# The expert passes' output stores are issued by GpSimd instead of the Activation engine

## The chip, the cores and the metric

The kernel runs on one core of one Trainium2 chip. The metric is device time in microseconds (us), the median of three runs. TensorE (PE) does the matmuls, VectorE (DVE) and the Activation engine (ACT) the elementwise work, GpSimd (POOL) some elementwise work and the indirect DMAs, and SyncE (SP) issues nearly all plain DMAs. All DMAs are carried by the same 16 DMA engines of the core; the profile counts them by queue: q1 holds what SP issues, q10 what ACT issues, q0 what GpSimd issues.

## What is computed

One decoder layer on 512 tokens of 1024 features: a mixer (mLSTM heads beside sliding-window attention heads), a layer norm, a hierarchical mixture of experts, a second layer norm. The part that the change touches is the mixture of experts, after the routing has picked two of 32 experts for each token:

```python
    for e in range(N_EXPERTS):
        h = jax.nn.silu(xt @ w_exp_gate[e]) * (xt @ w_exp_up[e])
        out = out + combine[:, e:e + 1] * (h @ w_exp_down[e])
    return out.reshape(B, S, Dm)
...
        x = layer_norm(ALPHA * x + y, ln2_w[l], ln2_b[l])
```

Everything is float32. The three weight tensors of the experts (1 MB each for one expert) are 101 MB together, and each is read once.

## The kernel before

The span has two stages. In the first, up to about 268 us, the mixer, the first norm and the routing run. In the second the experts run in 13 passes, numbered 0 to 12 (`ORDER = "BBBABABACBBCC"`). A pass gathers up to 128 token slots and serves two experts (kinds A and B) or four (kind C). For each pass TensorE forms the gate and up products of all its experts (`gu_part`, L1094), ACT and DVE make the hidden tile `hid` (`pair_h`, L1107 and L1108), TensorE transposes it (`dn_t`) and forms the down products `yo` (`dn_mm`, L1125). TensorE runs a pass's down products behind the next pass's gate and up products.

The results of passes 0 to 10 go to a DRAM buffer `yd`: `y_store` copies the two halves of `yo` to a tile `y` on ACT (L1142), scaled by the routing weight, and stores `y` (512 KB) by a DMA (L1143). Ahead of pass 11, `y_gather` fetches each token's two rows from `yd` with eight indirect DMAs of GpSimd (L1150), and DVE adds them to the residual `x1` (L1152). The results of passes 11 and 12 do not go through DRAM. Behind the eight adds in DVE's order stand the hidden tile of pass 11 and half of the copies that make the input `xs` of pass 12 (L1013).

The weights come in through a ring of 16 tiles of 1 MB, `we` (and two smaller buffers used once). `prefetch` (L624) takes free ring tiles in order and issues the loads of the next pass's weights from SP, two of 512 KB for gate and up (L597) or one of 1 MB for down (L601). A load waits until TensorE has read what its ring tile held before. `release` gives a pass's tiles back in a fixed order.

Which semaphore a DMA uses sets a second wait. The program has eight semaphores, DMAHW0 to DMAHW7, for the DMAs that SP and ACT issue, and eight, DMASW0 to DMASW7, for GpSimd's. They are dealt out in turn, in program order, and the next DMA on a semaphore waits at its issuing engine until the one before on that semaphore has landed. SP's queue is in order: what stands behind a waiting load waits too.

Of the kernel before, what the change touches and what calls it, by code (L numbers as in the profile page):

```python
# [24 lines left out]
P = 128  # L25
# [54 lines left out]
def layer_kernel(ctx, tc, x, w_in, conv_w, conv_b, gate_bias, norm_w, sinks, w_out, ln1_w, ln1_b,  # L80
# [3 lines left out]
    V, A, G, TE, SP = nc.vector, nc.scalar, nc.gpsimd, nc.tensor, nc.sync  # L84
# [16 lines left out]
    def slot(name, dt=F32, pool=None):  # L101
        _, p_, n = pools[pool or ("front" if name in FRONT else "mix")]
        return p_.tile([P, n], dt, tag="s", name=name)
# [29 lines left out]
    yd = DR.tile([KEPT * P + 1, DM], F32, name="yd")  # L133
# [998 lines left out]
    def y_split(py, cs, yh, yl):  # L1132
        for u in range(2):
            us = slice(512 * u, 512 * u + 512)
            A.activation(yh[:, us], py[u], AF.Copy, scale=cs)
            V.scalar_tensor_tensor(yl[:, us], py[u], cs, yh[:, us], op0=OP.mult, op1=OP.subtract)
        return yh, yl

    def y_store(py, p):
        y = slot("y")[:, :DM]  # L1140
        for u in range(2):
            A.activation(y[:, 512 * u:512 * u + 512], py[u], AF.Copy, scale=cws[:, p:p + 1])  # L1142
        A.dma_start(yd[p * P:(p + 1) * P], y)  # L1143


    def y_gather():
# [7 lines left out]
    def y_slots():  # L1154
        return [slot(n, F32R)[:, :DM] for n in ("yh", "yl")]
# [353 lines left out]
    for n, t in (("eid", eid), ("cwt", cwt), ("idf", idf), ("rank", rank)):  # L1509
        show(n, t)  # L1510

    y_store(pys[0], 0)
    xs = taken(2, hn)
    for d in range(2):
# [3 lines left out]
    hn = ready(4)  # L1518
    pg2 = pass_gu(xs, 0, 2)
    y_store(pys[1], 1)  # L1520
    prev = None
    l2 = []
# [28 lines left out]
    with tc.manual_schedule(engines={ENG.PE}):  # L1551
        for p in range(2, NP - 1):
            release(p, False)
            if p > 2:
                release(p - 1, True)
            prefetch(99)
            early = p in EARLY
            if early:
                y_store(pass_dn(dn_t(prev), p - 1), p - 1)
                y_gather()  # L1560
            hts = []
            pg = pg2 if p == 2 else pass_gu(xs, p % 2, p, (lambda: hts.append(dn_t(prev))) if prev and not early else None)
            if hts:
                ht = hts[0]
            h = pair_h(pg)
            if p % 2:
                xs = taken(p + 1, hn)
                if p + 3 < NP:
                    hn = ready(p + 3)
            if prev and not early:  # L1570
                y_store(pass_dn(ht, p - 1), p - 1)
            prev = h
# [45 lines left out]
    p = NP - 1  # L1618
# [4 lines left out]
    with tc.manual_schedule(engines=MAN):  # L1623
# [26 lines left out]
        y = y_split(py, cws[:, p - 1:p], *y_slots())  # L1650
# [133 lines left out]
```

## Time and profile before

| | |
|---|---|
| time, median of 3 runs (lowest, highest) | 553.78 us (550.93, 553.79) |
| time of the profiled execution | 549.58 us |
| its span from first to last instruction | 547.7 us |
| busy: PE, PEld, DVE, ACT, POOL | 478.3, 311.9, 257.3, 162.5, 146.5 us |
| DMA: read, written, mean rate | 128.68 MB, 10.49 MB, 254 GB/s |
| stores of `y` in q10 | 11 of 512 KB, 5.77 MB |

All times of events below are in us from the start of the span. The profiled execution lies 4.2 us under the median. Busy time alone does not show what a stage waits for: between 268 and 520 us the DMA engines move near their highest rate, and TensorE's busy share varies with what has been loaded. PEclk is the clock granted to TensorE, in tenths of its full 2.4 GHz.

### The profile page before, as it was taken

Reading aid. Unit: us, or ns where it says so; the run is one execution under the profiler, and the core shown is the slowest. Engines: PE = TensorE matmul, PEld = TensorE weight load, DVE = VectorE, ACT = ScalarE, POOL = GpSimd, SP = SyncE. Lnnn points to the kernel's source line nnn. Section 1 sums busy time; section 2 is a strip of 40 time slices with the busy share of each in tenths; the row PEclk is TensorE's granted clock in tenths of the full one; section 3 lists DMA queues with packets and bytes.
Section 4 is the critical chain, followed back from the end, with each engine's and each line's share of the span. In section 5 each row is a group of like instructions: output and inputs, shape, how many; then the busy total and the mean of one; then the engine's idle time right before and its main releaser. Section 6 shows DMA issues by size and latency. Waiting matters only on the chain. (4 is left out here: it accounts for less than half of the span.)

```text
span 547.7 us, 8113 instructions
## 1 busy us (share of the span) xinstructions
PE 478.3 (87%) x2904; PEld 311.9 (57%) x2904; DVE 257.3 (47%) x589; ACT 162.5 (30%) x352; POOL 146.5 (27%) x167
## 2 busy tenths in 40 slices
PE   6999899999999999797899999969478997287991
PEld 6998688798989878586447333216012631043330
DVE  3543898964487755978661103003000300324784
ACT  3552475874542512333202112202010211010520
POOL 4489724302311104646502000000000003201361
PEclk9999999999999999987999999989876997577996
DMA  8644213205936553759298998999799998999904
GB/s 229 198 117 116 78 34 94 77 30 158 414 89 185 193 149 133 276 193 376 80 394 323 405 425 335 394 390 373 245 418 333 404 347 307 411 421 413 424 29 172
DMA packets 44906, 139.42 MB, mean 255 GB/s; under 512 B 6386, under 2 KB 17674, under 8 KB 41024
## 3 DMA queue, kind: packets, MB, share of 16 engines
q1 hardware_dynamic: 40944, 126.05, 63.2%
q0 software_dynamic: 2336, 7.07, 3.5%
q10 hardware_dynamic: 1584, 5.77, 2.6%
q8 instruction: 24, 0.39, 0.3%
q14 instruction: 18, 0.15, 0.1%
HBM read 128.68 MB, written 10.49 MB: 254 GB/s over the span
## 5 line engine op out<-in xcount | busy, mean ns | idle before, releaser
L1094 PE MATMUL pg<-we,xs 128*32 128x512 f32 (+1 forms) x608 | 125.6, 674 | 33.7 <-DMA we<-in_w_exp_up 33.7
L1094 PEld LDWEIGHTS pg<-we,xs 128*32 128x32 f32 (+1 forms) x608 | 30.5, 129 | 114.2 <-issue 103.4
L245 PE MATMUL pj<-wh,xh 128*128 128x256 f32 (+1 forms) x224 | 63.2, 285 | 1.3 <-ACT wh L190 1.3
L246 PE MATMUL pj<-wh,xl 128*128 128x256 f32 (+1 forms) x224 | 62.4, 281 | 0.0
L1117 DVE COPY ht<-ph 128x256 f32<-128x256 f32 x13 | 5.5, 423 | 106.7 <-PE ph L1115 106.7
L250 PE MATMUL pj<-wl,xh 128*128 128x256 f32 x192 | 52.5, 280 | 0.0
L1150 POOL DMA_INDIRECT yg<-yd,yrow x8 | 7.5, 937 | 163.0 <-DMA yd<-y 153.5
L1125 PE MATMUL yo<-we,ht 128*32 128x512 f32 (+1 forms) x304 | 47.4, 595 | 2.1 <-DVE ht L1117 1.5
L1107 ACT ACTIVATE hid<-pg 128x256 f32<-128x256 f32 x13 | 5.0, 384 | 149.1 <-PE pg L1094 142.3
L1007 PE MATMUL xp<-ohr,x1h 128*128 128x256 f32 (+1 forms) x160 | 41.3, 297 | 5.9 <-DVE xs L1013 3.6
L245 PEld LDWEIGHTS pj<-wh,xh 128*128 128x128 f32 x224 | 42.1, 188 | 1.5 <-ACT wh L190 1.5
L246 PEld LDWEIGHTS pj<-wh,xl 128*128 128x128 f32 x224 | 42.1, 188 | 0.0
L1007 PE MATMUL xp<-ohr,x1l 128*128 128x256 f32 (+1 forms) x160 | 40.4, 292 | 0.0
L1007 PEld LDWEIGHTS xp<-ohr,x1h 128*128 128x128 f32 x160 | 32.2, 201 | 10.4 <-issue 5.2
L250 PEld LDWEIGHTS pj<-wl,xh 128*128 128x128 f32 x192 | 35.6, 188 | 0.0
L1007 PEld LDWEIGHTS xp<-ohr,x1l 128*128 128x128 f32 x160 | 32.3, 202 | 0.0
L191 DVE TENSOR_TENSOR wl<-wraw,wh 128x1024 fp32r<-128x1024 f32 x14 | 20.3, 1464 | 23.8 <-ACT wh L190 23.8
L1125 PEld LDWEIGHTS yo<-we,ht 128*32 128x32 f32 (+1 forms) x304 | 14.4, 119 | 29.0 <-issue 24.5
L190 ACT ACTIVATE wh<-wraw 128x1024 fp32r<-128x1024 f32 (+2 forms) x23 | 23.2, 1021 | 12.8 <-PE pj L246 4.2
L1152 DVE TENSOR_TENSOR x<-x,yg 128x1024 f32<-128x1024 f32 x8 | 9.9, 1239 | 35.1 <-DMA yg<-yd,yrow 35.1
L194 PE MATMUL pj<-xh,wh 128*128 128x512 f32 x64 | 25.7, 402 | 0.0
L196 PE MATMUL pj<-xl,wh 128*128 128x512 f32 x64 | 25.5, 399 | 0.0
(362 smaller groups left out, 913.5 us busy)
## 6 DMA issues: line engine op xcount, KB each, us to landing
we<-in_w_exp_gate SPq DMA_DIRECT2D x64, 512.0 KB
we<-in_w_exp_up SPq DMA_DIRECT2D x64, 512.0 KB
we<-in_w_exp_down SPq DMA_DIRECT2D x30, 1024.0 KB
wraw<-in_w_in SPq DMA_DIRECT2D x20, 512.0 KB
yd<-y ACTq DMA_DIRECT2D x11, 512.0 KB
xc<-in_x SPq DMA_DIRECT2D x4, 512.0 KB
wo<-in_w_out SPq DMA_DIRECT2D x8, 256.0 KB
wo<-in_w_out SPq DMA_DIRECT2D x4, 512.0 KB
```

Of the source, the lines that this page charges most:

```text
L190: A.activation(hi, src, AF.Copy)
L191: eng.tensor_tensor(lo, src, hi, op=OP.subtract)
L194: TE.matmul(o, lh, rh, start=start, stop=False)
L196: TE.matmul(o, lh, rl, start=False, stop=stop)
L245: TE.matmul(o, xh[j // 2][:, j % 2, cs], ws[i][j][0], start=j == 0, stop=False)
L246: TE.matmul(o, xl[j // 2][:, j % 2, cs], ws[i][j][0], start=False, stop=False)
L250: TE.matmul(o, xh[k // 2][:, k % 2, cs], ws[i][k][1], start=False, stop=k == 7)
L1007: TE.matmul(p_[:, j2, 0:P * n], w[c][:, 2 * g + j2], o[:, c, 0:P * n], start=c == 0 and s == 0 and j2 == 0, stop=c == NCH - 1 and s == 1 a ...
L1094: TE.matmul(pg[s:s + n], xs[k // 4][:, k % 4, P * b + s:P * b + s + n], ws[e][k // 4][:, :, k % 4], start=k == 0, stop=k == 7)
L1125: TE.matmul(py[u][s:s + n], ht[:, j, s:s + n], wt[e][2][j][:, 512 * u:512 * u + 512], start=j == 0, stop=j == 1)
L1150: G.indirect_dma_start(out=t, out_offset=None, in_=yd[:, :], in_offset=bass.IndirectOffsetOnAxis(ap=yrow[:, 2 * c + k:2 * c + k + 1], axis=0))
L1152: V.tensor_add(x1[c], x1[c], t)
```

## The change

One word: the DMA of L1143 is issued from GpSimd's queue (`G`) instead of ACT's (`A`).

```diff
@@ -1140,7 +1140,7 @@
         y = slot("y")[:, :DM]
         for u in range(2):
             A.activation(y[:, 512 * u:512 * u + 512], py[u], AF.Copy, scale=cws[:, p:p + 1])
-        A.dma_start(yd[p * P:(p + 1) * P], y)
+        G.dma_start(yd[p * P:(p + 1) * P], y)
```

On GpSimd, in the stretch from the last work of the first stage to the final norm, the eleven stores now stand between and behind the four gathers `xg<-xd` (the input rows of passes 4 to 7) and ahead of the eight gathers `yg<-yd`:

```order
 L1508 TENSOR_SCALAR x_2227<-x_2227 128x1024
-L1050 DMA xg<-xd,row 128x1024 x4
+L1143 DMA yd<-y 128x1024
+L1050 DMA xg<-xd,row 128x1024 x2
+L1143 DMA yd<-y 128x1024
+L1050 DMA xg<-xd,row 128x1024 x2
+L1143 DMA yd<-y 128x1024 x9
 L1150 DMA yg<-yd,yrow 128x1024 x8
 L1535 TENSOR_TENSOR l2d<-l2w,pcol 16x512 x2
```

The two gathers `xg` of passes 6 and 7 moved behind the second store, and the gathers `yg` stay behind all of them. Nothing else of GpSimd moved.

On SP no instruction moved, but the semaphores did. These are SP's loads of pass 3's down weights and of pass 4's gate and up weights, before; the wait named on a load is for the earlier DMA on its own semaphore and for TensorE's last read of the ring tile:

```order
L597 DMA we<-in_w_exp_up 128x1024 [waits DMAHW6_49]
L601 ISA
L601 DMA we<-in_w_exp_down 128x2048 [waits DMAHW0_49,PE_49]
...
L597 DMA we<-in_w_exp_gate 128x1024 [waits DMAHW5_49,PE_49]
L597 ISA
L597 DMA we<-in_w_exp_up 128x1024 [waits DMAHW6_49]
L597 ISA
L597 DMA we<-in_w_exp_gate 128x1024 [waits DMAHW7_49,PE_49]
```

The same loads in the changed kernel:

```order
L597 DMA we<-in_w_exp_up 128x1024 [waits DMAHW6_49]
L601 ISA
L601 DMA we<-in_w_exp_down 128x2048 [waits DMAHW7_49,PE_49]
...
L597 DMA we<-in_w_exp_gate 128x1024 [waits DMAHW3_49,PE_49]
L597 ISA
L597 DMA we<-in_w_exp_up 128x1024 [waits DMAHW4_49]
L597 ISA
L597 DMA we<-in_w_exp_gate 128x1024 [waits DMAHW5_49,PE_49]
```

Before, the first down load takes DMAHW0 right behind an up load on DMAHW6: DMAHW7 went to a store of ACT in between, and the last gate load shown is the next on DMAHW7. In the changed kernel SP's loads take the eight semaphores in turn without a gap, so a load waits for an earlier load of SP.

## Rows read from the trace of the kernel before

**Rows 1.** The page's slices of the span (40 slices; PE's busy share and PE's clock in tenths, DMA share in tenths, GB/s).

```profile
PE   6999899999999999797899999969478997287991
PEclk9999999999999999987999999989876997577996
DMA  8644213205936553759298998999799998999904
```

**Rows 2.** Waits of SP's queue from 268 to 510 us: line, what it waited for, total us, times, longest us.

```profile
SPq L597 <- DMA yd<-y: 59.7, 6, 12.7
SPq L597 <- DMA we<-in_w_exp_down: 31.9, 13, 4.0
SPq L601 <- DMA yd<-y: 10.6, 2, 7.3
SPq L597 <- PE pg L1094: 7.4, 5, 3.0
SPq L601 <- PE pg L1094: 3.2, 2, 1.9
```

**Rows 3.** SP's DMA issues around three of its stops, in order of time: start, length, what.

```profile
283.26 0.33 SPq L597 DMA_DIRECT2D we<-in_w_exp_up  x1
296.47 0.33 SPq L597 DMA_DIRECT2D we<-in_w_exp_gate  x1
...
301.08 4.20 SPq L601 DMA_DIRECT2D we<-in_w_exp_down  x2
...
378.11 0.33 SPq L597 DMA_DIRECT2D we<-in_w_exp_gate  x1
389.63 0.33 SPq L597 DMA_DIRECT2D we<-in_w_exp_up  x1
...
448.03 0.47 SPq L597 DMA_DIRECT2D we<-in_w_exp_up  x1
457.80 0.33 SPq L597 DMA_DIRECT2D we<-in_w_exp_gate  x1
```

**Rows 4.** The stores' issues on ACT that belong to them, and the last one.

```profile
288.35 0.35 ACTq L1143 DMA_DIRECT2D yd<-y  x1
383.04 0.33 ACTq L1143 DMA_DIRECT2D yd<-y  x1
448.87 0.33 ACTq L1143 DMA_DIRECT2D yd<-y  x1
453.49 0.33 ACTq L1143 DMA_DIRECT2D yd<-y  x1
```

**Rows 5.** Stretches of the span: stretch, its length, busy us of PE, PEld, DVE, ACT and POOL, PE's clock, DMA share, GB/s.

```profile
296.00:308.00 12.00, 12.00 (x81) 4.67 (x83) 1.11 (x2) 1.79 (x4) 1.87 (x2) 1.00 0.87 301
336.00:348.00 12.00, 11.77 (x65) 4.84 (x57) 4.51 (x12) 2.93 (x5) 0.00 (x0) 1.00 0.87 303
384.00:400.00 16.00, 8.48 (x36) 1.44 (x28) 0.00 (x0) 0.00 (x0) 0.00 (x0) 0.77 0.77 273
412.00:420.00 8.00, 6.26 (x16) 1.52 (x16) 0.00 (x0) 0.00 (x0) 0.00 (x0) 0.50 0.83 282
444.00:448.00 4.00, 4.00 (x20) 1.15 (x16) 0.42 (x1) 1.07 (x2) 0.00 (x0) 1.00 0.91 340
456.00:468.00 12.00, 7.11 (x28) 1.62 (x28) 0.00 (x0) 0.00 (x0) 4.69 (x5) 0.71 0.84 292
476.00:520.00 44.00, 35.05 (x195) 16.68 (x196) 21.86 (x38) 8.79 (x16) 7.89 (x10) 0.82 1.02 420
```

**Rows 6.** PE in order of time, with its idle time before and what ended it: passes 2 and 3 from 297.40, pass 9's gate and up products (to 421.49), pass 10's down products (449.08), pass 12's first gate and up products.

```profile
297.40 12.37 PE L1094 MATMUL pg<-we,xs 128*64 128x512 f32 x80
...
411.11 1.94 PE L1094 MATMUL pg<-we,xs 128*64 128x512 f32 x2 [3.69 <-DMA we<-in_w_exp_up]
414.78 6.24 PE L1094 MATMUL pg<-we,xs 128*64 128x512 f32 x16 [1.74 <-DMA we<-in_w_exp_up]
421.49 1.90 PE L1094 MATMUL pg<-we,xs 128*64 128x512 f32 x6 [0.47 <-DMA we<-in_w_exp_up]
...
449.08 3.65 PE L1125 MATMUL yo<-we,ht 128*64 128x512 f32 x16 [0.56 <-ACT y L1142]
...
500.54 1.71 PE L1094 MATMUL pg<-we,xs 128*32 128x512 f32 x2 [0.57 <-DMA we<-in_w_exp_up]
502.99 1.88 PE L1094 MATMUL pg<-we,xs 128*32 128x512 f32 x10 [0.74 <-DMA we<-in_w_exp_up]
```

**Rows 7.** The gathers of `yg` on GpSimd (first and last of eight), DVE's adds (first and last of eight) and what follows them, and PE's picks for pass 12 that wait for them.

```profile
460.03 0.94 POOL L1150 DMA_INDIRECT yg<-yd,yrow  x1 [153.51 <-DMA yd<-y]
476.09 0.94 POOL L1150 DMA_INDIRECT yg<-yd,yrow  x1 [1.62 <-DVE x L1152]
...
469.49 1.23 DVE L1152 TENSOR_TENSOR x<-x,yg 128x1024 f32<-128x1024 f32 x1 [20.51 <-DMA yg<-yd,yrow]
492.63 1.33 DVE L1152 TENSOR_TENSOR x<-x,yg 128x1024 f32<-128x1024 f32 x1 [2.50 <-DMA yg<-yd,yrow]
493.88 0.41 DVE L1108 TENSOR_TENSOR hid<-hid,pg 128x256 f32<-128x256 f32 x1
...
494.68 0.33 PE L1007 MATMUL xp<-ohr,x1h 128*128 128x128 f32 x1 [3.62 <-DVE xs L1013]
```

**Rows 8.** Plain DMAs that GpSimd issues already, and the landing times of its gathers: the 256 KB load of `csa` near the start (length of its issue in ns), then min/median/max us to landing of that load, of the `xg` gathers and of the `yg` gathers.

```profile
L172 POOL DMA_DIRECT2D csa<-in_mlstm_norm_w x1: 569/569/569, 23.6 to 23.6; - x1
...
DMA to landing us min/median/max: 3.4/3.4/3.4
...
DMA to landing us min/median/max: 8.9/8.9/9.5
...
DMA to landing us min/median/max: 9.4/13.3/16.4
```

## The prediction

> **What bounds the kernel now.** I read the slices of the page first: from the 21st of the 40 slices on, the DMA row stands at 9 with a few dips to 8 or 7, and PE's row falls to 4 and to 7 and 2 where the DMA row dips, in the 29th and around the 34th slice [rows 1]. So the expert stage runs at the pace of the weight loads, and the question is why the loads ever pause. The waits of SP's queue answer that: of all its waits between 268 and 510 us the longest sum is not for a free ring tile (7.4 + 3.2 = 10.6 us for PE) but for the stores of `y`: 59.7 + 10.6 = 70.3 us in 8 stops [rows 2]. Waits for earlier loads (31.9 us for the down loads) are harmless, since then the engines are full.
>
> The issue times show what such a stop is. SP issued a load at 283.26 and the next at 296.47 [rows 3]. In between ACT issued the store of pass 0, at 288.35 [rows 4]. SP's next load stands on the semaphore that went to that store, so it had to wait first until the store's data existed (5 us), then until it landed (8 us). The other two stops shown are alike: SP stood from 378.11 to 389.63 for a store issued at 383.04, and from 448.03 to 457.80 for one issued at 448.87. SP's queue is in order, so the whole weight stream stands behind TensorE's progress and a store's round trip. About 8 loads are under way when a stop begins; when they have landed, the DMA engines run dry.
>
> What the dry time costs is read from the stretches [rows 5]. Without a stop the engines move 420 GB/s (476 to 520 us). In each stretch at or behind a stop, length x (1 - rate/420) gives the time lost:
>
> - 296 to 308 at 301 GB/s: 3.4 us
> - 336 to 348 at 303: 3.3 us
> - 384 to 400 at 273: 5.6 us
> - 412 to 420 at 282: 2.6 us
> - 444 to 448 at 340: 0.8 us
> - 456 to 468 at 292: 3.7 us
>
> Together 19.4 us. The remaining stop, at a down load (the 7.3 us in [rows 2]), empties nothing that I can see and is left at zero.
>
> **The change, part by part.** *ACT loses 11 DMA issues* of about 0.33 us [rows 4], 3.6 us in all. ACT waits for TensorE in this stage anyway, so I count nothing for it.
>
> *GpSimd gains 11 issues.* The nearest rows are 0.57 us for its plain load of 256 KB and 0.94 us for a gather of 512 KB [rows 7, 8]. GpSimd sat idle for 153.51 us ahead of the first `yg` gather, so ten of them are hidden. It is in order: behind the first two stores stand the `xg` gathers of passes 4 to 7. The second pair goes out behind the store of pass 1, which ACT has ready before that pair could start anyway; their rows are used by TensorE passes later. I count nothing. The eleventh store is on a path (below): 0.94 - 0.33 = 0.6 us later.
>
> *The weight stream loses its eight stops.* The bytes stay the same, so what can come back is the 19.4 us, less what the ring takes. At the first stop it takes most. The four loads that follow (pass 4, second half) use tiles that TensorE frees when pass 1's down products end, near 290, so they go out some 6 us earlier than 296.47. But they are 2.1 MB, 5 us at 420 GB/s, and would end near 301. The load after them, issued at 301.08, takes tiles that pass 2's first half frees. That half cannot end before 297.40 + 2/7 of 12.37 = 300.9 [rows 3, 6]: TensorE does not move, and the dry time largely reappears behind 301. I let 1.0 of the 3.4 us count. From there the ring frees 2.1 MB every 3.6 us or so, against 5 us for their transfer, so tiles are free ahead of the loads, and I count the later stretches in full.
>
> *How it reaches the end.* Two chains meet at pass 12's gate and up products. One is the load stream itself: 1.0 + 3.3 + 5.6 + 2.6 + 0.8 + 3.7 = 17.0 us earlier. The other goes through the stores: TensorE waits for weights in pass 9 until 421.49, then runs nearly without a wait until pass 10's down products end at 452.7 [rows 6]; the last store goes out at 453.49, the gathers start at 460.03, DVE's last add starts at 492.63, and pass 11's hidden tile and pass 12's input stand behind it, for which PE waited 3.62 us [rows 7]. This chain moves with pass 9's weights, that is by the stops up to 420: 1.0 + 3.3 + 5.6 + 2.6 = 12.5 us. From it goes 0.6 us for GpSimd's issue. The landing of the last store took 460.03 - 453.49 = 6.5 us from ACT; from GpSimd the trace has no such store. The bounds are 3.4 us (a load half as large, with idle engines) and 9.5 us (a gather of the same size, with busy ones) [rows 8], so 3.1 us less to 3.0 us more; I take no difference, since the load beside it is like the gathers' but a store names no scattered rows. That leaves 11.9 us. In the kernel before, TensorE lost only 0.57 + 0.74 us to weights at pass 12 [rows 6], so the two chains were nearly level; with 11.9 against 17.0 the second one is late, and these waits go, which I leave as reserve. What follows pass 12's first products (some 45 us to the end of the span) does not change.
>
> The sum: 549.58 - 11.9 = 537.7 us against the profiled execution. The runs shown have their median 4.2 us higher, at 553.78, so the forecast for the median is 541.9 us.
>
> A rule speaks against all this. The Trainium skill, "DMA: Bandwidth & Descriptors", section "Issuing engines are not separate DMA queues", says that DMAs from any engine end up on the same 16 DMA engines and that spreading the issue over engines saves only the sequencer's own issue time. By it the sum would be nothing. The row that decides is SP's 70.3 us of waits for `yd<-y` [rows 2]: the stores do not slow the engines here, they stop the engine that issues the loads. The same page, section "Latency and other measured facts", gives about 1 us to the first byte for GpSimd's DMAs and 0.6 us for the others; by that the last store would land an estimated 0.4 us later.
>
> **The rivals.**
>
> *The stream gets everything back (534 to 538 us).* If the gathers also land sooner, because the loads of passes 11 and 12 were issued earlier and are partly done, the store chain does not bind and the 17.0 us of the load stream count: 536.8. Against it: the gathers took 9.4 to 16.4 us each among saturated loads [rows 8], and nothing thins them out.
>
> *The gathers give part of it back (545 to 551 us).* SP no longer stops at 448.03, so at the time of the gathers more loads stand in front of them. Each of the last three gathers waits for an add to free its tile, so landing times add up along the chain about three times; if they go from 13.3 to 15 us and the store lands at 9.5, 3 + 5 = 8 of the 12 us are gone: about 550.
>
> *Nothing changes (551.5 to 555.5 us).* Either a stop only stands in for a wait that the loads would meet anyway, or the ring's waits for PE take the place of each stop as at 301; then only ACT's 3.6 us of issue go, off the path. For it: the stream is close to its ceiling of 420 GB/s between the stops [rows 5]. Against it: PE is named for only 10.6 us of SP's waits [rows 2]. The skill's rule above comes out here.
>
> *Slower (over 556.5 us).* The place is again the chain from the last store to the last add, 453.49 to 493.96, 40.5 us. If the stores and gathers, now in one GpSimd queue, are starved by a stream that never pauses, it decides once this stretch exceeds 40.5 + 12.5 + 2.8 = 55.8 us. At 60 us the time would be 553.8 + 60 - 53 = 560.8. About four landings stand in series there (the store, and the gathers that wait for a tile), so each would have to take some 3.8 us longer; no row shows a gather above 16.4 us [rows 8].
>
> **How the numbers follow.** A measurement of this kernel tells about 0.5% (2.8 us) from no change. Chances: the forecast (538 to 545) 0.48, everything back 0.13, part given back 0.22, nothing 0.11, slower 0.06. The forecast's own range is 538 to 545 us. For 8 in 10 the range reaches down to 534 and up to 551, which leaves out the two last cases and the ends. Faster by over 0.5%: 0.48 + 0.13 + 0.22 = 0.83; within: 0.11; slower: 0.06.
>
> **What would show it.** In the profile after, SP's waits for `yd<-y` should be gone from the list, replaced by waits for earlier loads and some for PE. The DMA row should show one dip near 301 and no 7s between 380 and 470. q10 should vanish, and q0 grow by 5.77 MB. Pass 10's down products should end near 440 instead of 452.7, the first `yg` gather start near 448, and the last add end near 482. The prediction is wrong if SP's stops remain under another name with the same gaps in the GB/s, if the stretch from last store to last add grows by more than a few us, or if TensorE's pass 9 still waits for weights until 420.

## The result and the profile after

The changed kernel takes **538.7 us** (median of 4 runs, 537.38 to 538.84) against 553.78 (median of 4, 550.93 to 556.6) for the kernel before on the same chip: a ratio of 0.972, 95% interval 0.967 to 0.977. It is 15.1 us faster; the forecast was 11.9, and 538.7 lies inside the range of 534 to 551. Measured once more on another chip (below), the changed kernel was 12.5 us faster, a ratio of 0.978 (0.973 to 0.983).

The slices of the page after, and its rows for the weight wait, the stores and the queues (those of before are [rows 1]):

```profile
DMA  8624212220983539197559999999999999999504
...
q0 software_dynamic: 3920, 12.84, 6.3%
...
L1094 PE MATMUL pg<-we,xs 128*32 128x512 f32 (+1 forms) x608 | 114.0, 645 | 16.1 <-DMA we<-in_w_exp_up 16.1
...
L1143 POOL DMA_DIRECT2D yd<-y x11 | 6.1, 557 | 158.1 <-ACT y L1142 158.1
```

The DMA row has no dip left until the loads are done in the 38th slice. TensorE's wait for weights is 16.1 us (33.7 before). The stores now stand in q0; q10 is gone.

SP's waits after, from 268 to 510 us (line, what it waited for, total us, times, longest us), to set beside [rows 2]:

```profile
SPq L597 <- DMA we<-in_w_exp_down: 41.7, 20, 3.7
...
SPq L601 <- PE pg L1094: 10.6, 4, 8.7
SPq L597 <- PE pg L1094: 9.7, 5, 3.3
SPq L597 <- PE yo L1125: 6.5, 2, 6.0
```

The 70.3 us for `yd<-y` are gone. Most of the time SP now waits for an earlier load, as it should with full engines. The waits for a free ring tile have grown from 11.0 us (with two of 0.2) to 27.0 (with one of 0.2), but they empty little, as the stretches of [rows 5] show in the kernel after (the stage begins 3.9 us later in this execution, so the stretches are not exactly the same work):

```profile
296.00:308.00 12.00, 12.00 (x78) 7.37 (x76) 1.38 (x2) 2.09 (x4) 1.56 (x2) 1.00 1.02 404
...
336.00:348.00 12.00, 11.77 (x82) 4.99 (x76) 4.94 (x13) 2.93 (x5) 0.20 (x1) 1.00 1.02 410
384.00:400.00 16.00, 11.26 (x58) 2.52 (x60) 0.85 (x2) 0.39 (x1) 0.00 (x0) 0.79 1.02 421
...
412.00:420.00 8.00, 8.00 (x45) 4.14 (x42) 0.85 (x2) 0.72 (x2) 0.00 (x0) 0.99 1.01 419
444.00:448.00 4.00, 4.00 (x36) 0.94 (x32) 0.00 (x0) 1.12 (x2) 0.53 (x1) 1.00 1.03 418
456.00:468.00 12.00, 9.16 (x59) 4.78 (x58) 2.45 (x2) 0.38 (x1) 4.16 (x6) 0.78 1.01 423
```

The largest loss that is left lies between them: 376 GB/s from 363.51 to 383.51 us, which is 2.1 us against 420. The ring isn't its cause (SP waits for PE for 0.4 us between 350 and 385, and the DMA share is 1.00); the cause is open.

**Where the time came from.** The profiled spans differ by only 11.0 us (547.7 and 536.7). To compare stages I count from the first full block of gate and up products, which begins the expert stage. It starts at 269.62 in the kernel before and at 273.51 in the kernel after. The 3.9 us between them come from the first stage, where the change touches nothing; it varies from one execution to another (271.25 in a second profile of the same kernel, below). First before, then after: that block, and the issue of the last four weight loads; for the kernel before also the first products of pass 12 and their transpose.

```profile
269.62 8.80 PE L1094 MATMUL pg<-we,xs 128*64 128x512 f32 x40
504.20 4.69 SPq L601 DMA_DIRECT2D we<-in_w_exp_down  x4
...
497.93 2.05 PE L1094 MATMUL pg<-we,xs 128*32 128x512 f32 x4
...
504.80 0.50 PE L1115 MATMUL ph<-ident,hid 128*128 128x128 f32 x2
```

```profile
273.51 8.80 PE L1094 MATMUL pg<-we,xs 128*64 128x512 f32 x40
488.02 5.46 SPq L601 DMA_DIRECT2D we<-in_w_exp_down  x4
```

The end of the load stream moved from 234.6 us behind the start of the stage to 214.5, by 20.1 us. The other chain, in the kernel after (GpSimd's last store and first gather; DVE's first and last add; TensorE's products of pass 12 and their transpose):

```profile
445.59 0.53 POOL L1143 DMA_DIRECT2D yd<-y  x1 [4.08 <-ACT y L1142]
454.08 0.98 POOL L1150 DMA_INDIRECT yg<-yd,yrow  x1 [7.97 <-issue]
...
462.72 1.23 DVE L1152 TENSOR_TENSOR x<-x,yg 128x1024 f32<-128x1024 f32 x1 [21.91 <-DMA yg<-yd,yrow]
...
482.78 1.23 DVE L1152 TENSOR_TENSOR x<-x,yg 128x1024 f32<-128x1024 f32 x1 [1.27 <-DMA yg<-yd,yrow]
...
488.34 3.09 PE L1094 MATMUL pg<-we,xs 128*32 128x512 f32 x16
491.36 0.50 PE L1115 MATMUL ph<-ident,hid 128*128 128x128 f32 x2
```

With [rows 4], [rows 6] and [rows 7] this gives, from the start of the stage:

| | before | after | earlier by |
|---|---|---|---|
| last store issued | 183.9 | 172.1 | 11.8 |
| first `yg` gather | 190.4 | 180.6 | 9.8 |
| last add begins | 223.0 | 209.3 | 13.7 |
| pass 12's transpose begins | 235.2 | 217.9 | 17.3 |
| end of the span | 278.1 | 263.2 | 14.9 |

So the stage itself is 14.9 us shorter, close to the 15.1 between the medians. These are single profiles: in the second one of the changed kernel the stage takes 266.3 us, 11.8 less than before.

### The profile page after: what moved, and what is told of

It reads as the page before. It is cut to its first block, busy times and chain, and to the rows that moved or that the text cites. A ratio compares the mean times of both kernels' runs of the same rounds, so it can differ in the third digit from the quotient of the medians.

```text
span 536.7 us, 8111 instructions
## 1 busy us (share of the span) xinstructions
PE 472.7 (88%) x2904; PEld 315.7 (59%) x2904; DVE 260.8 (49%) x589; ACT 163.1 (30%) x352; POOL 152.4 (28%) x178
## 5 line engine op out<-in xcount | busy, mean ns | idle before, releaser
L1094 PE MATMUL pg<-we,xs 128*32 128x512 f32 (+1 forms) x608 | 114.0, 645 | 16.1 <-DMA we<-in_w_exp_up 16.1
L1094 PEld LDWEIGHTS pg<-we,xs 128*32 128x32 f32 (+1 forms) x608 | 29.0, 127 | 86.9 <-issue 74.0
L1007 PE MATMUL xp<-ohr,x1h 128*128 128x256 f32 (+1 forms) x160 | 45.0, 314 | 18.3 <-ACT xs L1015 8.8
L1143 POOL DMA_DIRECT2D yd<-y x11 | 6.1, 557 | 158.1 <-ACT y L1142 158.1
L1007 PEld LDWEIGHTS xp<-ohr,x1h 128*128 128x128 f32 x160 | 34.6, 217 | 22.9 <-ACT xs L1015 8.9
L1007 PE MATMUL xp<-ohr,x1l 128*128 128x256 f32 (+1 forms) x160 | 44.1, 309 | 0.0
L1007 PEld LDWEIGHTS xp<-ohr,x1l 128*128 128x128 f32 x160 | 35.0, 219 | 0.0
L195 PE MATMUL pj<-xh,wl 128*128 128x512 f32 x64 | 26.3, 411 | 0.0
## 6 DMA issues: line engine op xcount, KB each, us to landing
we<-in_w_exp_gate SPq DMA_DIRECT2D x64, 512.0 KB, 11.8
```

What stands on the lines that cost most here:

```text
L195: TE.matmul(o, ll, rh, start=False, stop=False)
L1007: TE.matmul(p_[:, j2, 0:P * n], w[c][:, 2 * g + j2], o[:, c, 0:P * n], start=c == 0 and s == 0 and j2 == 0, stop=c == NCH - 1 and s == 1 a ...
L1094: TE.matmul(pg[s:s + n], xs[k // 4][:, k % 4, P * b + s:P * b + s + n], ws[e][k // 4][:, :, k % 4], start=k == 0, stop=k == 7)
L1143: G.dma_start(yd[p * P:(p + 1) * P], y)
```

## The experiments

The store on ACT with 4 KB, the two halves and the first measurement of the moved adds ran on one chip beside the kernel before (556.33 us there); the others ran on a second chip (555.27 us). "The start" below is again the first full block of the expert stage, at 274.33 (a token on ACT), 274.01 (early), 275.40 (late), 273.96 (first store), 273.57 (last store), and 274.50 and 269.69 us (adds moved, two profiles).

**The stores on GpSimd, and a 4 KB store on ACT behind each.** This separates which queue carries the bytes from who holds a semaphore. It adds a DRAM tile `yt` and, at L1143:

```diff
         G.dma_start(yd[p * P:(p + 1) * P], y)
+        A.dma_start(yt[p:p + 1], y[0:1])
```

> The changed kernel, with one small DMA more per pass: behind each store on GpSimd, ACT writes one row of y (4 KB) to a DRAM buffer of its own. The full stores stay on GpSimd; the small DMA takes the semaphore between SP's loads that the store took in the kernel before. Theory (SP stops because a load stands on the semaphore of a DMA that ACT cannot issue yet): the stops are back, SP's waits name yt for 40 to 70 us in all, and the time is near the kernel before, 546 to 555 us where that takes 553.8 (a small DMA may land sooner than a full store, which gives some of it back). Rival (the gain is that 5.77 MB left ACT's queue, or that GpSimd's queue carries them better): 538 to 540 us, as the changed kernel.

Measured: 550.85 us, ratio 0.991 (0.987 to 0.995). 5.5 us of gain are left, about a third of what the change gives. SP's waits in this kernel, and its last weight loads:

```profile
SPq L597 <- DMA yt<-y: 44.9, 7, 9.5
...
SPq L601 <- DMA yt<-y: 6.1, 2, 5.3
```

```profile
498.87 3.91 SPq L601 DMA_DIRECT2D we<-in_w_exp_down  x4
```

The big stores are still in q0, and eleven DMAs of 4 KB bring 51.0 of the 70.3 us of SP's waits back. The last load goes out 224.5 us behind the start, half way between after (214.5) and before (234.6). Most of the cost is therefore the semaphore that the store takes, with the time until its data exist and have landed, and not its 512 KB. The third of the gain that is left goes with shorter stops (51.0 us instead of 70.3); whether the bytes in ACT's queue have a part in it isn't separated.

**The early or the late half alone.** `(G if p < 6 else A)` moves the stores of passes 0 to 5, `(A if p < 6 else G)` those of passes 6 to 10:

```diff
-        G.dma_start(yd[p * P:(p + 1) * P], y)
+        (G if p < 6 else A).dma_start(yd[p * P:(p + 1) * P], y)
```

> Only the stores of passes 0 to 5 go to GpSimd, those of passes 6 to 10 stay on ACT. Theory (each stop costs what the DMA engines lose behind it): 1.0 + 3.3 us of the stretches up to 348 come back, about 4 us, less if the ring's lead covers them: 549 to 552 us where before takes 553.8. Rival (each moved store is worth the same): 6/11 of 15.1 us = 8.2, 545.6 us.

> The other half: the stores of passes 0 to 5 stay on ACT, those of passes 6 to 10 go to GpSimd. Theory: the stretches from 384 on come back, 5.6 + 2.6 us on the chain of the stores, 3.7 and 0.8 more on the stream, and with the shorter wait at pass 12 some 9 to 12 us: 542 to 545 us where before takes 553.8. Rival (each moved store is worth the same): 5/11 of 15.1 = 6.9, 546.9 us.

Measured: early 550.56 us, ratio 0.990 (0.982 to 0.998), 5.8 us faster than before; late 548.84, ratio 0.987 (0.979 to 0.996), 7.5 us faster. First early, then late: SP's waits for stores that remain, and the last loads.

```profile
SPq L597 <- DMA yd<-y: 34.6, 4, 9.5
```

```profile
502.13 4.40 SPq L601 DMA_DIRECT2D we<-in_w_exp_down  x4
```

```profile
SPq L597 <- DMA yd<-y: 21.8, 2, 11.5
...
SPq L601 <- DMA yd<-y: 10.8, 2, 7.1
```

```profile
495.38 3.98 SPq L601 DMA_DIRECT2D we<-in_w_exp_down  x4
```

The last load goes out 228.1 us behind the start with the early half moved, 6.5 earlier than before, and 220.0 with the late half, 14.6 earlier. The two add up to 21.1, near the 20.1 of the full change. Stores of equal worth would have given about 11 and 9 of the 20.1, so on the load stream the rival fails. The times decide nothing: the early half's interval reaches from 1 to 10 us, which holds both 4.3 and 8.2; the late half's 7.5 us lie below the 9 to 12 that were expected and near the rival's 6.9, and its interval, 2 to 12 us, holds both. In the stream the early half is worth more than the 4.3 us of the prediction's terms.

**Only the first store back on ACT.** This measures the first stop, of which the prediction let 1.0 us count.

```diff
-        G.dma_start(yd[p * P:(p + 1) * P], y)
+        (A if p == 0 else G).dma_start(yd[p * P:(p + 1) * P], y)
```

> Only the store of pass 0 is back on the Activation engine; the other ten stay with GpSimd. SP should stand once, for yd<-y, from about 284 to 297 us (some 12 us), at the place of the first stop of the kernel before. The prediction's step: the ring would have taken most of this stop's gain anyway, so the kernel loses 1.0 us against the changed one. Rival: the stop is worth its full dry time, 3.4 us or more (the ring's waits in the changed kernel, 27 us of PE in SP's waits, stand beside full DMA engines and cost nothing). The experiment with the early half on GpSimd suggests the rival: there 5.7 us came back for the first half, where the prediction's terms give 4.3. Read from the length of the expert stage (from the first x40 block of gate and up products to the end of the span): 263.2 us in the changed kernel; 264.2 by the step, 266.6 or more by the rival.

Measured: 544.28 us, against 542.74 for the changed kernel on the same chip (below). The 1.5 us between them cannot be told from nothing. The length of the stage, named beforehand as the yardstick, does not decide either: it is 267.8 us here, and 263.2 and 266.3 in the two profiles of the changed kernel. The load stream is sharper. The one stop in SP's list, and SP's issues around it:

```profile
SPq L597 <- DMA yd<-y: 6.7, 1, 6.7
```

```profile
294.13 0.33 SPq L597 DMA_DIRECT2D we<-in_w_exp_gate  x1
301.32 0.33 SPq L597 DMA_DIRECT2D we<-in_w_exp_up  x1
```

The stop stands one load later than expected and is shorter (6.7 us instead of 12). What it costs is read from the same stretch of the stage, 20 to 50 us behind the start, in the kernel before, in the kernel after and in this one:

| kernel | stretch (us) | DMA share | GB/s |
|---|---|---|---|
| before | 289.62 to 319.62 | 0.96 | 369 |
| after | 293.51 to 323.51 | 1.02 | 413 |
| first store on ACT | 293.96 to 323.96 | 0.97 | 383 |

Against the changed kernel this one loses 30 x (413 - 383)/420 = 2.1 us, and the kernel before 3.1 us. The five other profiles without a store on ACT in this stretch (the second one of the changed kernel, the early half, both with the adds moved, and the one with the last store alone on ACT, below) have 412 to 416 GB/s. So the rival was right on the stream, though its price came out at 2.1 us instead of 3.4. How much of that reaches the last store is less clear: it goes out 175.1 us behind the start here, and at 172.1 to 173.8 in the five profiles in which no store on ACT stands before it, so 1.3 to 3.1 us earlier.

**Only the last store back on ACT.** This asks whether GpSimd's queue is why the last store lands later.

```diff
-        G.dma_start(yd[p * P:(p + 1) * P], y)
+        (A if p == KEPT - 1 else G).dma_start(yd[p * P:(p + 1) * P], y)
```

> Only the last store (pass 10) is back on the Activation engine. By the queue theory its landing (store issued to first gather) falls from 8.5 us to the 6.5 us of the kernel before, so the chain of stores, gathers and adds ends 2 us earlier; the one stop of SP that it brings back (some 10 us, with 0.8 + 3.7 = 4.5 us of lost transfer) falls on the load stream, which had about 2.3 us in hand, so pass 12 waits for weights again and the whole is 1 to 3 us slower than the changed kernel. Rival: the landing is set by the loads beside it and not by the issuing queue, so it stays near 8.5 us; then the whole is also 2 to 4 us slower, but without the earlier first gather.

Measured: 545.28 us, 2.5 more than the changed kernel beside it, which again cannot be told from nothing (ratios 0.981 and 0.978, intervals of 0.005 to either side). SP stops once; ACT's store and the first gather:

```profile
441.43 0.33 SPq L597 DMA_DIRECT2D we<-in_w_exp_gate  x1
452.56 0.33 SPq L597 DMA_DIRECT2D we<-in_w_exp_up  x1
...
447.41 0.35 ACTq L1143 DMA_DIRECT2D yd<-y  x1
...
453.33 0.98 POOL L1150 DMA_INDIRECT yg<-yd,yrow  x1 [9.74 <-DMA yd<-y]
```

From the store to the first gather it took 5.9 us, as the queue theory said. The chain did not end earlier for it, though: the last add begins 211.5 us behind the start, in the changed kernel 209.3 and 210.7. Pass 12 waits for weights again, as expected: from its first product to its transpose it takes 5.7 us instead of 3.0. And the store fell into the stop that it made itself, with the engines at 151 GB/s between 447 and 454 us. Two stores of another run have the same queue and different traffic. In the experiment with 4 KB stores GpSimd issued the store of pass 9 at 446.95, 3.5 us behind SP's last load before a stop (443.42; the next goes out at 450.92), and that of pass 10 at 451.57, behind the loads that followed. Their landing times, in that order:

```profile
L1143 POOL DMA_DIRECT2D yd<-y x1: 531/531/531, 447.0 to 447.0; - x1
...
DMA to landing us min/median/max: 5.6/5.6/5.6
...
L1143 POOL DMA_DIRECT2D yd<-y x1: 533/533/533, 451.6 to 451.6; - x1
...
DMA to landing us min/median/max: 9.3/9.3/9.3
```

And the traces of the two halves have ACT's landing for five stores. In the late half, those of passes 1, 4 and 5 took 7.8, 9.0 and 7.8 us; from GpSimd in the changed kernel they took 7.2, 7.4 and 8.0. In the early half, those of passes 7 and 9 took 6.7 and 8.4, from GpSimd 7.3 and 7.9. GpSimd's queue is therefore not slower, pass for pass, and one queue alone spreads from 5.6 to 9.3 us. That speaks for the rival, that the loads beside a store set its landing, but only a few stores show it, and a small part for the queue isn't excluded.

**The adds behind pass 12's input.** `y_gather()` moves from ahead of pass 11 to behind the lines of the loop that make pass 12's input, so that DVE's hidden tile of pass 11 and the copies of `xs` no longer stand behind eight adds. This takes the store chain off pass 12, and the load stream alone is left.

```diff
-                y_gather()
...
+            if early:
+                y_gather()
```

> The changed kernel with y_gather called behind pass 12's input instead of ahead of pass 11, so that DVE and ACT make pass 11's hidden tile and pass 12's input before the adds of yg. Theory (the chain of last store, gathers and adds sets when pass 12's products start, 488.3 us in the profile after, while its weights are there some 8 us earlier): pass 12 starts near 480, and the time is 5 to 8 us under the changed kernel, 531 to 534 us where that takes 538.7. Rival (the load stream itself binds pass 12): within 1.5 us of 538.7.

Measured: 537.8 us, ratio to before 0.964 (0.952 to 0.976). By the ratio of the changed kernel (0.972), that would be some 4.5 us less than it, short of the 5 to 8 that were expected, and the intervals overlap. So it was run again beside the changed kernel itself:

> The kernel with the gathers and adds moved behind pass 12's input, once more, beside the changed kernel on the same chip. If the chain of stores, gathers and adds was the bound of the changed kernel with 2 to 3 us over the load stream, this one is 2 to 3 us faster than the changed kernel. If the two chains are level, it is within 1 us.

> The changed kernel itself, once more, as the common yardstick of this series on the same chip: ratio to the kernel before 0.967 to 0.977, that is 12.7 to 18.3 us faster. A second profile of it shows which of its numbers repeat: the landing of the last store (8.5 us), the last add (120.5 us behind... read from the start of the expert stage, 210.5 us), the ring's waits on SP (27 us).

Measured on that chip: the changed kernel 542.74 us (538.68 to 543.97, 6 runs), ratio 0.978 (0.973 to 0.983), just outside the 0.967 to 0.977 that were expected; with the adds moved 536.37 us (533.61 to 539.93, 6 runs), ratio 0.969 (0.963 to 0.974). The version with the adds moved is the fastest of this study, 6.4 us under the changed kernel beside it and 4.5 by the first ratios: more than either forecast, 2 to 3 us and 1 us, though the intervals still touch. TensorE at pass 12 in its second profile:

```profile
474.19 1.88 PE L1094 MATMUL pg<-we,xs 128*32 128x512 f32 x2 [6.97 <-DMA we<-in_w_exp_up]
479.18 1.91 PE L1094 MATMUL pg<-we,xs 128*32 128x512 f32 x2 [3.10 <-DMA we<-in_w_exp_up]
...
498.39 1.92 PE L1094 MATMUL pg<-we,xs 128*32 128x512 f32 x16
```

TensorE has pass 12's input early (it starts 204.5 us behind the start, 214.8 in the changed kernel) and waits for weights, four times (twice more, 1.2 and 0.6 us, in the rows left out). So in this version the load stream is the bound, and in the changed kernel the adds were. The products of pass 12 end only a little earlier for it: their transpose begins 218.6 us behind the start here (215.5 in its first profile), 217.9 and 219.4 in the changed kernel. The two chains lie within some 2 us of each other. A part of the rest is in the last block above: 1.92 us here, and in the changed kernel

```profile
501.71 3.22 PE L1094 MATMUL pg<-we,xs 128*32 128x512 f32 x16
```

which comes back to the clock below.

The second profile of the changed kernel repeats the first in the expert stage: last store 172.6 us behind the start, last add 210.7, ring waits 25.9 us, last store to first gather 9.0 instead of 8.5. Only its end comes 3.1 us later.

## Why the prediction was right, and where its steps were off

**The cause was right.** The stores stopped SP by its semaphores. Take them off these semaphores and every stretch of [rows 5] runs at 404 to 423 GB/s; put a 4 KB DMA on them and most stops are back. One premise was too wide: the stage does not run at the pace of the loads from its start. The store of pass 5 goes out 85.1 to 85.4 us behind the start in all ten profiles, whichever stores make SP stop. Up to there TensorE keeps its own pace, and a stop only uses up the lead of the loads; from pass 6 on the stores come apart (113.4 us before, 105.6 after). The rule weighed against the change (the Trainium skill, "DMA: Bandwidth & Descriptors", section "Issuing engines are not separate DMA queues") allows only the issue time as a gain. The measured 15.1 us disagree, with 3.6 us of issue on ACT.

**The first stop: the step that was off.** The prediction let 1.0 of 3.4 us count, since the ring would stop SP again at the same place. SP did stop there, and to the tenth of a us where it was forecast; the stretch behind it stands below:

```profile
295.71 0.34 SPq L597 DMA_DIRECT2D we<-in_w_exp_up  x1
304.96 0.98 SPq L601 DMA_DIRECT2D we<-in_w_exp_down  x2
...
300.00:308.00 8.00, 8.00 (x44) 3.37 (x43) 0.69 (x1) 1.29 (x3) 1.56 (x2) 1.00 1.02 397
```

304.96 less the 3.89 us by which the stage starts later is 301.07, and [rows 3] have 301.08. But the engines did not run dry: they moved 397 GB/s from 300 to 308 us. The prediction gave the four loads 5 us from their issue, so that they "would end near 301". The second of them went out at 294.25 and landed 11.5 us later, at 305.75, and two more stood behind it: the engines still had work when the load behind the stop went out at 304.96. A second stop was also overlooked. The pair of down loads at 301.08 lasts 4.20 us in [rows 3] and 0.98 here, because its second load had waited 3.3 us for a store (the smaller of the two waits of L601 in [rows 2]). The stretches from 20 to 50 us behind the start put the two stops together at 3.1 us, of which 2.1 are the first; the prediction's 1.0 was 2.1 us too small.

**The load stream.** Forecast 17.0 us earlier, measured 20.1 and, in the second profile, 18.4. Early half 6.5 instead of 4.3, late half 14.6 instead of 12.7. The two stops at the start explain 2.1 us of this (3.1 instead of 1.0). The rest lies late, where the chosen stretches were too short: from 429.62 to 469.62 the kernel before moves 349 GB/s, which is 6.8 us lost against 420, and the prediction's two stretches there add up to 4.5. Against this stands the 2.1 us lost from 363.51 to 383.51 in the kernel after, of which no term knew; the kernel before loses 0.5 in the same part of the stage (359.62 to 379.62, 410 GB/s).

**The chain to the adds.** The chain up to the last store was forecast 11.9 us earlier (12.5 less 0.6 for GpSimd's longer issue). The store came 11.8 and 11.3 earlier, and its issue took 0.53 us instead of 0.33. That this fits is partly luck: the term of the first stop was 2.1 us too small, and the surplus does not show here. In the kernel after TensorE waits for pass 9's weights for the last time at

```profile
407.57 7.66 PE L1094 MATMUL pg<-we,xs 128*64 128x512 f32 x22 [1.90 <-DMA we<-in_w_exp_up]
```

This is the third product of pass 9, 134.1 us behind the start. The same product before is the row of 414.78 in [rows 6], at 145.2, and there a last wait followed at 151.9. So pass 9 gained 11.1 us at this product and 12.1 at the transpose behind its products (423.33 before, 415.16 after). From there on TensorE ran without a wait for weights, to pass 10's down products, which end at 444.6. That its own pace kept the surplus of the loads from the store is read from this place alone.

The landing, taken from the store's issue to the first gather and held to be unchanged, grew from 6.5 to 8.5 and 9.0 us, inside the bound of 3.0. About 1.0 us of the 8.5 lies behind the landing itself (7.5 us). The latency that the Trainium skill gives for GpSimd's DMAs ("DMA: Bandwidth & Descriptors", section "Latency and other measured facts") would make an estimated 0.4 us of the growth; no run here separates that from the spread within one queue (5.6 to 9.3). The gathers, also taken as unchanged, went the other way: from the first gather to the last add 32.6 us became 28.7 (29.1 in the second profile). So the fear behind the second rival, gathers that slow down because SP never pauses, had the wrong sign.

**The reserve at pass 12.** The prediction found 0.57 + 0.74 = 1.3 us of waits for weights in [rows 6] and left them out. They were larger. From the first product of pass 12 to its transpose it took 504.80 - 497.93 = 6.9 us before and 491.36 - 488.34 = 3.0 after, for the same 16 matmuls. The rows of x4 with 2.05 us (above) and x2 with 1.71 [rows 6] hide waiting inside their length; the idle time beside a row is only the part between the groups. This gave 3.6 us from the last add to the transpose that the sum did not have.

**The tail.** Taken as unchanged at some 45 us, from the transpose to the end it was 42.9 us before and 45.3 after (46.9 in the second profile). A part of it is one block of 16 products, which takes 3.22 us after (the row above) and took 1.93 before:

```profile
514.83 1.93 PE L1094 MATMUL pg<-we,xs 128*32 128x512 f32 x16
```

TensorE's granted clock is lower there. The stretch in which TensorE had nothing to do, and that of the block, in the kernel after:

```profile
480.00:484.00 4.00, 0.00 (x0) 0.00 (x0) 2.44 (x3) 0.00 (x0) 0.14 (x1) 0.50 1.03 421
...
500.00:504.00 4.00, 4.00 (x18) 1.27 (x20) 3.63 (x9) 2.77 (x5) 2.04 (x5) 0.62 0.78 330
```

0.50 is the lower level, 1.2 GHz. The clock had risen to 1.00 between 492 and 500 us and fell again, though TensorE was busy for 3.6 of every 4 us there. With the adds moved (second profile) it is 1.00 from 492 to 508 us and the block takes 1.92 us. Among the ten profiles the block is slow (3.2 to 3.6 us) in six and takes 1.9 in four: before, the early half, and both with the adds moved. From pass 12's transpose to the next one it is 24.1 to 24.2 us in the six and 22.5 to 22.6 in the four, so the slower block accounts for some 1.6 us of the tail. From that next transpose to the end the ten scatter between 20.4 and 23.3 us, with no pattern that I see. Why the clock falls in one and not in the other I did not settle.

**The sum.** -11.8 for the last store, +2.0 landing, -3.9 gathers, -3.6 pass 12, +2.4 tail: -14.9. The forecast had the first term and none of the others. Two errors of 3.6 and 3.9 us helped, two of 2.0 and 2.4 hurt, and they left 3 us: that the forecast is so near is in part luck. The time fell between the forecast (541.9) and the top of the first rival's range (538); its condition, gathers that land sooner, was partly met, though loads stood beside them throughout.

## What to carry to other kernels

Look at what the queue that issues the critical loads waits for, by name. If it waits for a DMA of another engine with which it has no data in common, look whether the two share a completion semaphore: here a store of 4 KB could stop a stream of 512 KB loads. Issuing the store where it takes no such semaphore was worth most of the dry time behind the stops, as far as the loads, and not TensorE, set the pace there. When two chains meet late in a kernel, compute both, and move the one that has become the bound: here the adds behind the next pass's input gave 4.5 to 6.4 us more.

## What was unexpected on the chip

The gathers of `yg` come in at two steady paces. The adds follow each other by 2.5 us (472.70, 475.21, 477.74 us after) or by 3.7 (462.72, 466.44, 470.18), in both kernels; for 0.524 MB that is 210 and 140 GB/s, a half and a third of the 420 that the engines move. In the kernel before the half comes first and in the kernel after the third, and the total changes with how many gathers fall in which. What stands beside them in each case (gate and up loads, or down loads, which have longer rows) would be a cause: in the kernel after the slower pace ends at about 470 us, where the last of four down loads lands (issued at 451.31, 19.4 us to landing). It was not tried. A plain store from GpSimd costs its queue 0.53 to 0.68 us, less than the 0.94 of a gather by which the prediction bounded it, and in the changed kernel it lands in 6.8 to 8.6 us; ACT's five with a landing time take 6.7 to 9.0.
